# An mLSTM/Fourier backbone: adaLN weight loads, their products and h's tiles re-ordered in the first stage

## The chip, the cores and the metric

The kernel runs on 1 core of one Trainium2 chip, in one launch. The metric is device time in microseconds (us), from the runs of the whole program; the program before takes 1016.68 us (median of 3 runs, 1015.91 to 1017.34).

## The reference, cut to what matters

Two layers over 512 latent tokens `x` with a prefix of 256 context tokens `ctx`, width D = 1024, E = 2048. Everything is float32. The change touches only what leads to the input `h` of layer 0 and what shares its stage:

```python
sc_lat, sc_ctx = silu(c), silu(c_ctx)
sh, sc, g = split(sc_lat @ w_ada[0] + b_ada[0], 3)        # adaLN: shift, scale, gate; w_ada[0] is 1024 x 3072
h  = rmsnorm(x,   norm_g[0]) * (1 + sc)  + sh             # 512 x 1024
hc = rmsnorm(ctx, norm_g[0]) * (1 + scc) + shc            # 256 x 1024, from sc_ctx
xm, o_pre, z = split(h @ w_in, 3)                         # w_in: 1024 x 6144
q = einsum('bnhd,hde->bhne', xconv, w_q)                  # 4 heads of 512
k = einsum('bnhd,hde->bhne', xconv, w_k) * 512 ** -0.5
```

Behind it come the mLSTM scan in both directions, the output map, and a Fourier layer.

## The kernel before, in words

Matrix products in float32 are made of three products of rounded halves (`hi` x `hi`, `hi` x `lo`, `lo` x `hi`); `split` writes both halves of a tile (line 106 casts, line 107 subtracts).

The program's first stage, called M here, needs no token. For each head it forms M = w_q w_k^T / sqrt(512), so that q and k are never formed by themselves. It runs 16 steps `i` = (head h, quarter et). A step issues, in this order: at et = 3 `fold_sum(h)` (16 small products with gate weights); `turn` of the *next* step (8 TensorE transposes of w_q and w_k, copied by ScalarE, split by VectorE and POOL); then `product(h, et)` (12 matmuls of 128x512, lines 371 and 372). After each of the 12 matmuls `side_step` lets one piece of a list of side jobs run: `fold_turn` (4 transposes), `ada_done` (8 transposes), `h_tile(k)` (6 transposes of token tiles in two pieces, scale and shift by ScalarE, `split` of the context half and the latent half), `open_wp` (first weight split of the next stage).

Other work sits behind a step's product: `gate_weights` (8 transposes of m_w_if), `params` (3 transposes of the small vectors; it makes silT = silu(c), which the adaLN products read), `ada_part` (16 products of 4 rows of w_ada with silT, line 272; one half of the K range of one half of the 2048 columns, so four `ada_part` in all), the squares and norms of the tokens. Behind M comes stage X (`x_cols`, lines 497 to 504), which multiplies h with w_in and needs all eight h tiles in its first pass.

Loads: `sy.dma_start` runs on SyncE's queue (SP), in program order. A DMA takes one of eight semaphores, DMAHW0 to DMAHW7, and waits at its issue until the semaphore's last user has landed; a DMA into a buffer in use also waits there for the engine that reads the buffer. What stands behind waits too. The tag `wraw` has two buffers, which hold m_w_if first, then pieces of 1 MB of w_ada, then pieces of w_in; `adw` is one more buffer of 1 MB. w_q and w_k have two buffers per head.

The order of PE, DVE, ACT and POOL is that of the program text (`manual_schedule`); the order of SP is a scheduler's.

Of the kernel before, what the change touches and what calls it, by code (L numbers as in the profile page):

```python
# [9 lines left out]
F32 = mybir.dt.float32  # L10
# [14 lines left out]
H = 4  # L25
# [40 lines left out]
def hybrid_kernel(ctx: ExitStack, tc: tile.TileContext, I, out):  # L66
# [110 lines left out]
    def load_q(h, between=None):  # L177
        w = {nm: A1.tile([P, 4, DH], F32, tag=f"w{nm}", bufs=2, name=f"w{nm}") for nm in "qk"}
        for s_ in (slice(0, P), slice(P, 2 * P), slice(2 * P, DH)) if h == 0 else (slice(0, DH),):
            for nm in "qk":  # L180
                sy.dma_start(out=w[nm][:, :, s_], in_=I[f"m_w_{nm}"][0, h].rearrange("(t p) e -> p t e", p=P)[:, :, s_])
                if between:
                    between()
        wqk[h] = {nm: [w[nm][:, t] for t in range(4)] for nm in "qk"}
# [17 lines left out]
    bif = edge[0:NR, 2:4]  # L202
    gp.memset(bif, 0.0)

    def load_small(n):
        for _ in range(n):
            dst, src = rows_in.pop(0)
            sy.dma_start(out=dst, in_=src)
# [4 lines left out]
        for i in range(6):  # L213
            sy.dma_start(out=xs[i], in_=I["ctx"][0, i * P:(i + 1) * P, :] if i < 2 else I["x"][0, (i - 2) * P:(i - 1) * P, :])

    def ada_load(half, part):
        w = []
        for k in range(4 * part, 4 * part + 4, 2):
            if len(w) == 0 and part == 1:
                t = A2.tile([P, 2, D], F32, tag="adw", bufs=1, name="adw")  # L220
            else:
                t = wraw().rearrange("p (a k) c -> p a (k c)", a=2)
            sy.dma_start(out=t, in_=I["w_ada"][0, k * P:(k + 2) * P, half * D:(half + 1) * D].rearrange("(a p) c -> p a c", p=P))
            w += [t[:, 0], t[:, 1]]
            load_small(min(3, len(rows_in)))
        return w

    NG, BA, CB, LW, SK, CW = 16, 32, 80, 96, 112, 128

    def params():  # L230
# [65 lines left out]
    def h_tile(k):  # L296
        pl, pc = ps("gt", 2), tp()
        for i in range(2):
            tr(pc[:, i * P:(i + 1) * P], xs[i][:, k * P:(k + 1) * P])
        raw = A2.tile([P, NT], F32, tag="hraw", bufs=3, name="hraw")  # L300
        sc.activation(out=raw[:, 0:NCX], in_=pc[:, 0:NCX], func=AF.Identity,
                      scale=acol[:, 1, k, 1:2], bias=acol[:, 0, k, 1:2])
        for i in range(4):
            tr(pl[:, i * P:(i + 1) * P], xs[2 + i][:, k * P:(k + 1) * P])
            if i == 1:
                yield
        sc.activation(out=raw[:, NCX:], in_=pl, func=AF.Identity,
                      scale=acol[:, 1, k, 0:1], bias=acol[:, 0, k, 0:1])
# [50 lines left out]
    def side_step():  # L359
        while side and next(side[0], side) is side:  # L360
            side.pop(0)

    def product(h, et):

        if et == 0:
            pm[h] = [mm() for _ in range(4)]
        q, k = T.pop((h, "q", et)), T.pop((h, "k", et))
        for dt in range(4):
            c = slice(dt * P, (dt + 1) * P)
            for j, (l, r) in enumerate(((q[0], k[0]), (q[0], k[1]), (q[1], k[0]))):  # L370
                te.matmul(pm[h][dt], lhsT=l[:, c], rhs=r, start=(et == 0 and j == 0), stop=(et == 3 and j == 2))  # L371
                side_step()
        if et == 3:
            for dt in range(4):
                mst = A1.tile([P, DH], F32, tag="mst", bufs=4, name="mst")
                sc.activation(out=mst, in_=pm[h][dt], func=AF.Copy, scale=DH ** -0.5)
                m_st.append((h, dt, mst))
# [23 lines left out]
                         op=ALU.add, axis=mybir.AxisListType.X)  # L401
        yield

    load_q(1, lambda: load_small(3))
    st_st = ExitStack()
    st_st.enter_context(tc.manual_schedule(engines=ENGINES))
    w_in = I["m_w_in"][0]
    aw = {}
    warm = edge[:, 1:2]
    sc.activation(out=warm, in_=nhalf, func=AF.Sigmoid)  # L410
    b1_st, b2_st, b3_st = ExitStack(), ExitStack(), ExitStack()
# [1 line left out]
    def open_wp():  # L413
        nonlocal WP, w_bufs, w_first, w_split
        a2_st.close()
        WP = pool("WP", "left", stack=b1_st)
        w_bufs = 2
        w_split = wsplit([w_first[:, :, q * P:(q + 1) * P] for q in range(2)])
        w_first = [next(w_split)]
        yield  # L420

    steps = [(h, et) for h in range(H) for et in range(4)]
    turn(0, 0)
    for i, (h, et) in enumerate(steps):
        if et == 3:
            fs = fold_sum(h)
        if i + 1 < len(steps):
            turn(*steps[i + 1])
        if et == 3:
            side.append(fold_turn(h, fs))  # L430
        product(h, et)
        if et == 0:
            m_store()
        if i == 0:
            aw[0] = ada_load(0, 0)
            load_q(2)
        elif i == 1:
            gate_weights()
        elif i == 3:
            params()  # L440
        elif i == 4:
            ada_part(0, aw[0])
            aw[1] = ada_load(0, 1)
            load_x()
        elif i == 7:
            ada_part(1, aw[1])
            load_q(3)
            aw[2] = ada_load(1, 0)
            side.append(ada_done(0))
        elif i == 11:  # L450
            ada_part(0, aw[2])
            aw[3] = ada_load(1, 1)
            w_first = wraw()
            sy.dma_start(out=w_first, in_=w_in[:, 0:256].rearrange("(k p) c -> p k c", p=P))
            sy.dma_start(out=cst[:, P:], in_=I["cst"][:, P:])
            for r in range(2):
                for j, nm in enumerate(("m_b_i", "m_b_f")):
                    sy.dma_start(out=bif[32 * r:32 * r + H, j:j + 1], in_=I[nm][0, r, :].unsqueeze(1))
        elif i == 12:
            ada_part(1, aw[3])  # L460
            side.append(ada_done(1))
            side.extend(h_tile(k) for k in range(KD))
            side.append(open_wp())
        for j in {7: (0, 1), 8: (2,), 9: (3, 4), 10: (5,)}.get(i, ()):
            token_square(j)
        if i == 10:
            rstd_of(rs, ss, 1.0 / D)
        elif i in (11, 12):
            token_norms(3 * i - 33)
    m_store()  # L470
    while side:
        side_step()
# [1070 lines left out]
```

## Time and profile before

| | us |
|---|---|
| median of 3 runs | 1016.68 |
| lowest, highest | 1015.91, 1017.34 |
| the profiled execution | 1012.39 |
| its span, first to last instruction | 1010.6 |
| TensorE (PE) busy in the span | 982.0 (97%) |
| VectorE (DVE) busy | 736.4 (73%) |
| ScalarE (ACT) busy | 435.5 (43%) |
| POOL (GpSimd) busy | 137.0 (14%) |

How to read it: times inside the program are us from the span's start. The profiled execution took 1.8 us more than its span and 4.3 us less than the median of the runs. A row of the timeline gives start, busy time, engine, line, output <- inputs, how many, and in brackets how long the engine idled before and on whom. Matmuls overlap, so from one start to the next is the time that each costs. M runs from 0 to the first matmul of line 497.

### The profile page before, as it was taken

Reading aid. Unit: us, or ns where it says so; the run is one execution under the profiler, and the core shown is the slowest. Engines: PE = TensorE matmul, PEld = TensorE weight load, DVE = VectorE, ACT = ScalarE, POOL = GpSimd, SP = SyncE. Lnnn points to the kernel's source line nnn. Section 1 sums busy time; section 2 is a strip of 40 time slices with the busy share of each in tenths; the row PEclk is TensorE's granted clock in tenths of the full one; section 3 lists DMA queues with packets and bytes.
Section 4 is the critical chain, followed back from the end, with each engine's and each line's share of the span. In section 5 each row is a group of like instructions: output and inputs, shape, how many; then the busy total and the mean of one; then the engine's idle time right before and its main releaser. Section 6 shows DMA issues by size and latency. Waiting matters only on the chain.

```text
span 1010.6 us, 14164 instructions
## 1 busy us (share of the span) xinstructions
PE 982.0 (97%) x5231; PEld 805.5 (80%) x5231; DVE 736.4 (73%) x1303; ACT 435.5 (43%) x824; POOL 137.0 (14%) x126
## 2 busy tenths in 40 slices
PE   7999999999999998999999999999989999999997
PEld 6666888788888866787788888888868898988886
DVE  4558698898888757637888888775799876657623
ACT  2455434344344244236545455353666332325510
POOL 2003100000000000411535352110102101000000
PEclk9999999999999999999999999999999999999999
DMA  9963776657765474634354544453523443413602
GB/s 310 381 246 114 222 228 224 209 181 246 229 214 199 155 245 137 176 111 152 114 161 125 158 126 126 156 174 101 195 94 103 138 146 115 135 64 99 204 1 84
DMA packets 146893, 166.70 MB, mean 165 GB/s; under 512 B 15108, under 2 KB 107804, under 8 KB 146824
## 3 DMA queue, kind: packets, MB, share of 16 engines
q1 hardware_dynamic: 131172, 140.35, 43.9%
q10 hardware_dynamic: 15652, 25.45, 6.7%
q8 instruction: 41, 0.67, 0.3%
q14 instruction: 28, 0.23, 0.1%
HBM read 138.47 MB, written 27.30 MB: 164 GB/s over the span
## 4 chain that ended last, share of the span: by engine, by line
PE 73%; DVE 15%; issue 5%; ACT 3%; DMA 3%; POOL 1%; SPq 0%; ACTq 0%; POOLq 0%; DVEq 0%
PE mm L101 14%; PE mm L102 14%; PE mm L103 14%; PE tp L137 4%; PE mm L371 4%; PE gt L965 2%; PE mm L497 2%; PE mm L503 2%; PE mm L499 2%; PE gt L102 1%; PE gt L103 1%; PE gt L101 1%; PE mm L498 1%; PE mm L504 1%; PE mm L500 1%
## 5 line engine op out<-in xcount | busy, mean ns | idle before, releaser
L106 ACT CAST whi<-wraw 128x1024 fp32r<-128x1024 f32 x62 | 64.2, 1049 | 102.0 <-PE mm L102 42.3
L520 DVE SCALAR_TENSOR_TENSOR acc<-xm,pcol,acc 128x441 f32<-128x441 f32 (+2 forms) x128 | 89.0, 696 | 25.7 <-ACT acc L510 21.7
L107 DVE TENSOR_TENSOR wlo<-wraw,whi 128x1024 fp32r<-128x1024 f32 x60 | 76.0, 1280 | 41.3 <-ACT whi L106 39.9
L101 PE MATMUL mm<-hhi,whi 128*128 128x512 f32 x256 | 102.0, 398 | 1.3 <-ACT whi L106 1.3
L103 PE MATMUL mm<-hhi,wlo 128*128 128x512 f32 x256 | 100.4, 392 | 0.5 <-DVE wlo L107 0.5
L102 PE MATMUL mm<-hlo,whi 128*128 128x512 f32 x256 | 100.4, 392 | 0.0
L107 DVE TENSOR_TENSOR wol<-woraw,woh 128x512 fp32r<-128x512 f32 x80 | 55.1, 703 | 36.8 <-ACT woh L106 36.3
L102 PE MATMUL mm<-wol,yhi 128*128 128x512 f32 (+1 forms) x208 | 78.3, 376 | 2.1 <-DVE wol L107 2.1
L101 PE MATMUL mm<-woh,yhi 128*128 128x512 f32 (+1 forms) x208 | 78.5, 377 | 0.1
L103 PE MATMUL mm<-woh,ylo 128*128 128x512 f32 (+1 forms) x208 | 77.7, 373 | 0.0
L106 ACT CAST woh<-woraw 128x512 fp32r<-128x512 f32 x80 | 48.3, 619 | 42.9 <-PE mm L103 24.7
L101 PEld LDWEIGHTS mm<-hhi,whi 128*128 128x128 f32 x256 | 48.4, 189 | 13.5 <-ACT whi L106 1.7
L103 PEld LDWEIGHTS mm<-hhi,wlo 128*128 128x128 f32 x256 | 48.5, 189 | 11.5 <-DVE wlo L107 1.0
L102 PEld LDWEIGHTS mm<-hlo,whi 128*128 128x128 f32 x256 | 48.5, 189 | 9.4
L497 PE MATMUL mm<-hhi,whi 128*128 128x512 f32 x128 | 51.2, 400 | 0.0
L499 PE MATMUL mm<-hlo,whi 128*128 128x512 f32 x128 | 50.9, 398 | 0.0
L107 POOL TENSOR_TENSOR xhl<-st,xhh 128x768 fp32r<-128x768 f32 x16 | 34.5, 2171 | 114.3 <-ACT xhh L106 61.9
L101 PE MATMUL mm<-Zh,whi 128*128 128x512 f32 x128 | 50.0, 391 | 0.0
L102 PE MATMUL mm<-Zl,whi 128*128 128x512 f32 x128 | 50.0, 391 | 0.0
L103 PE MATMUL mm<-Zh,wlo 128*128 128x512 f32 x128 | 49.8, 389 | 0.0
L102 PEld LDWEIGHTS mm<-wol,yhi 128*128 128x128 f32 x208 | 39.2, 188 | 10.6 <-DVE wol L107 4.0
L503 PE MATMUL mm<-hhi,wlo 128*128 128x512 f32 x128 | 45.9, 398 | 0.0
(360 smaller groups left out, 2636.4 us busy)
## 6 DMA issues: line engine op xcount, KB each, us to landing
wraw<-in_m_w_in_dram SPq DMA_DIRECT2D x32, 512.0 KB, 6.5
adw<-in_w_ada_dram SPq DMA_DIRECT2D x32, 512.0 KB, 3.9
wraw<-in_f_w_in_dram SPq DMA_DIRECT2D x14, 1024.0 KB, 5.3
woraw<-in_m_w_out_dram SPq DMA_DIRECT2D x48, 256.0 KB, 2.8
wraw<-in_m_w_in_dram SPq DMA_DIRECT2D x8, 1024.0 KB, 5.6
g_d<-g ACTq DMA_DIRECT2D x32, 256.0 KB, 5.9
gg<-g_d SPq DMA_DIRECT2D x32, 256.0 KB, 2.7
woraw<-in_f_w_out_dram SPq DMA_DIRECT2D x32, 256.0 KB, 3.4
```

Of the source, the lines that this page charges most:

```text
L101: te.matmul(ps, lhsT=lh, rhs=rh, start=start, stop=False, **kw)
L102: te.matmul(ps, lhsT=lh, rhs=rl, start=False, stop=False, **kw)
L103: te.matmul(ps, lhsT=ll, rhs=rh, start=False, stop=stop, **kw)
L106: (sc.copy if he is None else he.tensor_copy)(out=hi, in_=src)
L107: (le or gp).tensor_tensor(out=lo, in0=src, in1=f32(hi), op=ALU.subtract)
L137: te.transpose(out_, in_=in_, identity=ident[0:n, 0:n])
L371: te.matmul(pm[h][dt], lhsT=l[:, c], rhs=r, start=(et == 0 and j == 0), stop=(et == 3 and j == 2))
L497: te.matmul(pl, lhsT=lh, rhs=hhi[k], start=(k == 0), stop=False)
L499: te.matmul(pl, lhsT=lh, rhs=hlo[k], start=False, stop=False)
L503: te.matmul(pl, lhsT=ll, rhs=hhi[k], start=False, stop=(k == KD - 1))
L520: ve.scalar_tensor_tensor(out=ag[:, r0:r1, o0:o1], in0=xg[:, r0 + dy:r1 + dy, o0 + dx:o1 + dx], scalar=tap(4 + 3 * dy + dx), in1=ag[:, r0: ...
L965: te.matmul(po, lhsT=k.ph[:, t], rhs=v, start=(t == 0 and v is s.v[0][0]), stop=False)
```

## The change

It does five things.

- Six products of a 128x128 tile of ones with itself run on PE at the very start (`WAKE`).
- The nine small loads go ahead of everything else behind m_w_if; then two pieces of w_ada; and only then w_q and w_k of head 1. `ada_load` loads one piece of 1 MB, not two, and is called where a buffer comes free.
- `gate_weights`, `params` and the four `ada_part` move to earlier steps: behind products 0, 1, and 2, 3, 5, 7 (before: 1, 3, and 4, 7, 11, 12). `ada_done` runs in steps 4 and 8 (before: 8 and 13).
- The eight `h_tile` run in steps 9 to 14 (before: 13 to 15), and the side jobs of a step are spaced evenly over its 12 matmuls, by their number `n`.
- All halves of h, and the `lo` half of the first w_in pieces, are written by DVE (before: half of the `lo` halves of h, and those of w_in, by POOL).

```diff
+WAKE = 6
...
     gp.memset(ones, 1.0)
+    awake = tp(P)
+    for _ in range(WAKE):
+        te.matmul(awake, lhsT=ones, rhs=ones, start=True, stop=True)
...
-    def ada_load(half, part):
-        w = []
-        for k in range(4 * part, 4 * part + 4, 2):
-            if len(w) == 0 and part == 1:
-                t = A2.tile([P, 2, D], F32, tag="adw", bufs=1, name="adw")
-            else:
-                t = wraw().rearrange("p (a k) c -> p a (k c)", a=2)
-            sy.dma_start(out=t, in_=I["w_ada"][0, k * P:(k + 2) * P, half * D:(half + 1) * D].rearrange("(a p) c -> p a c", p=P))
-            w += [t[:, 0], t[:, 1]]
-            load_small(min(3, len(rows_in)))
-        return w
-
+    def ada_load(half, part, i):
+
+        if part == 1 and i == 0:
+            t = A2.tile([P, 2, D], F32, tag="adw", bufs=1, name="adw")
+        else:
+            t = wraw().rearrange("p (a k) c -> p a (k c)", a=2)
+        k = 4 * part + 2 * i
+        sy.dma_start(out=t, in_=I["w_ada"][0, k * P:(k + 2) * P, half * D:(half + 1) * D].rearrange("(a p) c -> p a c", p=P))
+        aw.setdefault((half, part), []).extend((t[:, 0], t[:, 1]))
...
-        split(raw[:, 0:NCX], chi[k], clo[k], ve, ve if k % 2 else gp)
-        split(raw[:, NCX:], hhi[k], hlo[k], ve, gp if k % 2 else ve)
+        split(raw[:, 0:NCX], chi[k], clo[k], ve, ve)
+        split(raw[:, NCX:], hhi[k], hlo[k], ve, ve)
...
-    def product(h, et):
+    def product(h, et, n):
...
+        done = 0
...
                 te.matmul(pm[h][dt], lhsT=l[:, c], rhs=r, start=(et == 0 and j == 0), stop=(et == 3 and j == 2))
-                side_step()
+                while done < (3 * dt + j + 1) * n // 12:
+                    side_step()
+                    done += 1
+        while side:
+            side_step()
...
-    load_q(1, lambda: load_small(3))
+    load_small(9)
+    ada_load(0, 0, 0)
+    ada_load(0, 1, 0)
+    load_q(1)
...
-        w_split = wsplit([w_first[:, :, q * P:(q + 1) * P] for q in range(2)])
+        w_split = wsplit([w_first[:, :, q * P:(q + 1) * P] for q in range(2)], ve)
...
+    after = {
+        0: lambda: (gate_weights(), ada_load(0, 0, 1)),
+        1: lambda: params(),
+        2: lambda: (ada_first(0, 0), ada_load(0, 1, 1), ada_load(1, 0, 0), load_x()),
+        3: lambda: (ada_first(1, 0), ada_load(1, 0, 1), load_q(2), ada_load(1, 1, 0)),
+        5: lambda: (ada_first(0, 1), ada_load(1, 1, 1), [token_square(j) for j in range(3)]),
+        6: lambda: (load_q(3), [token_square(j) for j in range(3, 6)], rstd_of(rs, ss, 1.0 / D)),
+        7: lambda: (ada_first(1, 1), last_loads(), token_norms(0)),
+        8: lambda: token_norms(3),
+    }
+    turned = {9: (0,), 10: (1,), 11: (2,), 12: (3, 4), 13: (5,), 14: (6, 7)}
...
-        product(h, et)
+            n += 5
+        if i in (4, 8):
+            side.append(ada_done(i // 4 - 1))
+            n += 9
+        for k in turned.get(i, ()):
+            side.append(h_tile(k))
+            n += 2
+        product(h, et, n)
         if et == 0:
             m_store()
-        if i == 0:
-            aw[0] = ada_load(0, 0)
-            load_q(2)
-        elif i == 1:
-            gate_weights()
-        elif i == 3:
-            params()
-        elif i == 4:
-            ada_part(0, aw[0])
-            aw[1] = ada_load(0, 1)
-            load_x()
...
+        after.get(i, lambda: None)()
```

`ada_first(part, half)` calls `ada_part`; `last_loads` holds the loads of the first w_in piece and of the constants, which stood in the loop at i = 11.

What the change does to the order, in three places. Line numbers of the changed text are some 4 to 10 higher; a number behind a name is its buffer.

SP's queue, before, from the load of m_w_if on: `wq_159` and `wk_160` are w_q and w_k of head 1, `rows0` takes the small vectors, `wraw_232` is the first piece of w_ada.

```order
L189 DMA wraw_146<-in_m_w_if_dram 96x1024
L181 DMA wq_159<-in_m_w_q_dram 128x4x512
L208 DMA rows0_148<-in_c_dram 8x128
L208 DMA rows0_148<-in_c_ctx_dram 8x128
L208 DMA rows0_148<-in_norm_g_dram 16x128
L181 DMA wk_160<-in_m_w_k_dram 128x4x512
L208 DMA rows0_148<-in_b_ada_dram 48x128
L208 DMA rows0_148<-in_m_conv_b_dram 16x128
L208 DMA rows0_148<-in_m_ln_w_dram 16x128
L223 DMA wraw_232<-in_w_ada_dram 128x2x1024
```

The same queue in the changed kernel, from the fourth small load behind m_w_if on (`wraw_175`, `adw_177` and `wraw_261` are pieces of w_ada, `wq_179` and `wk_180` head 1):

```order
L212 DMA rows0_155<-in_b_ada_dram 48x128
L212 DMA rows0_155<-in_m_conv_b_dram 16x128
L212 DMA rows0_155<-in_m_ln_w_dram 16x128
L212 DMA rows0_155<-in_m_skip_dram 16x128
L212 DMA rows0_155<-in_m_conv_w_dram 128x128
L212 DMA rows0_155<-in_m_conv_w_dram 16x128
L227 DMA wraw_175<-in_w_ada_dram 128x2x1024
L227 DMA adw_177<-in_w_ada_dram 128x2x1024
L185 DMA wq_179<-in_m_w_q_dram 128x4x512
L185 DMA wk_180<-in_m_w_k_dram 128x4x512
L227 DMA wraw_261<-in_w_ada_dram 128x2x1024
L218 DMA xs0_158<-in_ctx_dram 128x1024
```

No large load stands between m_w_if and the last small one any more, and head 1 stands behind two pieces of w_ada.

PE, before, from the last matmul of product 2 on (`gt<-wqT,wif` is fold_sum, `tp<-cst,wq` the turn of step 4, which is head 1):

```order
L371 MATMUL mm<-wkTh,wqTl 128x512
L389 MATMUL gt<-wqT,wif 32x512 x4
L389 MATMUL gt<-wkT,wif 32x512 x4
L137 MATMUL tp<-cst,wq 128x128 x4
L137 MATMUL tp<-cst,wk 128x128 x4
```

PE in the changed kernel from the same matmul on:

```order
L375 MATMUL mm<-wkTh,wqTl 128x512
L275 MATMUL gt<-wraw,silT 32x512 x8
L397 MATMUL gt<-wqT,wif 32x512 x4
L397 MATMUL gt<-wkT,wif 32x512 x4
L138 MATMUL tp<-cst,wq 128x128 x4
L138 MATMUL tp<-cst,wk 128x128 x4
```

The first `ada_part`, which reads `wraw_175` and `wraw_261`, now stands ahead of fold_sum and of the turn of head 1.

PE in step 14, before: between two matmuls of the product stand pieces of `h_tile` (`xs`), a tile every second matmul.

```order
L371 MATMUL mm<-wkTh,wqTl 128x512
L137 MATMUL gt<-cst,xs_155 128x128
L137 MATMUL gt<-cst,xs_156 128x128
L371 MATMUL mm<-wkTh,wqTh 128x512
L137 MATMUL tp<-cst,xs_151 128x128
L137 MATMUL tp<-cst,xs_152 128x128
L137 MATMUL gt<-cst,xs_153 128x128
L137 MATMUL gt<-cst,xs_154 128x128
L371 MATMUL mm<-wkTl,wqTh 128x512
```

PE in the changed kernel, in step 12, one of the two steps with two tiles:

```order
L138 MATMUL tp<-cst,xs_158 128x128
L138 MATMUL tp<-cst,xs_159 128x128
L138 MATMUL gt<-cst,xs_160 128x128
L138 MATMUL gt<-cst,xs_161 128x128
L375 MATMUL mm<-wkTh,wqTh 128x512
L375 MATMUL mm<-wkTl,wqTh 128x512
L375 MATMUL mm<-wkTh,wqTl 128x512
L138 MATMUL gt<-cst,xs_162 128x128
L138 MATMUL gt<-cst,xs_163 128x128
L375 MATMUL mm<-wkTh,wqTh 128x512
L375 MATMUL mm<-wkTl,wqTh 128x512
L375 MATMUL mm<-wkTh,wqTl 128x512
```

Three matmuls stand between two pieces of a tile, and a tile takes six.

## Rows read from the trace of the kernel before

**Rows 1.** Windows: length, busy us by engine, granted PE clock, DMA share, GB/s.
```profile
20.00:60.00 40.00, 40.00 (x247) 28.02 (x246) 23.51 (x46) 19.87 (x37) 0.00 (x0) 1.00 1.00 389
95.00:96.00 1.00, 1.00 (x8) 0.00 (x0) 0.97 (x2) 0.00 (x0) 1.00 (x2) 0.50 0.00 0
```

**Rows 2.** Timeline of PE, regular steps of M and a late adaLN product.
```profile
56.74 0.60 PE L137 MATMUL tp<-cst,wq 128*128 128x128 f32 x4
...
59.93 0.39 PE L371 MATMUL mm<-wkTl,wqTh 128*128 128x512 f32 x1
60.15 0.39 PE L371 MATMUL mm<-wkTh,wqTl 128*128 128x512 f32 x1
60.47 1.06 PE L389 MATMUL gt<-wqT,wif 128*32 128x512 f32 x8
...
62.33 0.65 PE L137 MATMUL tp<-cst,wq 128*128 128x128 f32 x4
...
66.57 1.93 PE L272 MATMUL gt<-wraw,silT 128*32 128x512 f32 x16
...
72.22 1.05 PE L272 MATMUL gt<-adw,silT 128*32 128x512 f32 x4
...
76.18 0.66 PE L137 MATMUL tp<-cst,wq 128*128 128x128 f32 x4
```

**Rows 3.** Timeline of PE, the end of M and stage X.
```profile
80.33 0.38 PE L137 MATMUL tp<-cst,xs 128*128 128x128 f32 x2
...
85.01 0.38 PE L137 MATMUL tp<-cst,xs 128*128 128x128 f32 x2
...
86.14 0.38 PE L137 MATMUL tp<-cst,xs 128*128 128x128 f32 x2
...
93.05 1.94 PE L389 MATMUL gt<-wqT,wif 128*32 128x512 f32 x8 [1.82 <-ACT hraw L307]
...
96.49 0.50 PE L371 MATMUL mm<-wkTh,wqTh 128*128 128x512 f32 x1
...
100.14 0.39 PE L497 MATMUL mm<-hhi,whi 128*128 128x512 f32 x1
...
142.69 0.38 PE L498 MATMUL mm<-chi,whi 128*128 128x256 f32 x1 [0.40 <-ACT acc L510]
```

**Rows 4.** The tile hhi: durations in ns, min/median/max.
```profile
L106 DVE CAST hhi<-hraw x8: 418/472/1519, 82.2 to 98.1; 128x512 fp32r<-128x512 f32 x8
```

**Rows 5.** Timeline of SP's queue: when loads are issued.
```profile
11.97 0.31 SPq L208 DMA_DIRECT2D rows<-in_m_conv_b_dram  x1
13.41 0.31 SPq L208 DMA_DIRECT2D rows<-in_m_ln_w_dram  x1
15.75 0.39 SPq L223 DMA_DIRECT2D wraw<-in_w_ada_dram  x1
...
16.68 0.89 SPq L208 DMA_DIRECT2D rows<-in_m_conv_w_dram  x2
18.33 0.38 SPq L223 DMA_DIRECT2D wraw<-in_w_ada_dram  x1
...
21.10 0.37 SPq L181 DMA_DIRECT2D wk<-in_m_w_k_dram  x1
```

**Rows 6.** DMA issues between 33.0 and 33.5: size, us from issue to landing.
```profile
wraw<-in_w_ada_dram SPq DMA_DIRECT2D x1, 1024.0 KB, 5.1
```

**Rows 7.** Timeline of PE, the first steps of M.
```profile
10.26 0.63 PE L371 MATMUL mm<-wkTh,wqTh 128*128 128x512 f32 x1
10.69 0.53 PE L371 MATMUL mm<-wkTl,wqTh 128*128 128x512 f32 x1
...
16.30 1.02 PE L137 MATMUL gt<-cst,wraw 96*128 96x96 f32 x8
...
20.88 1.07 PE L389 MATMUL gt<-wqT,wif 128*32 128x512 f32 x8
...
26.89 0.54 PE L137 MATMUL tp<-cst,rows 128*128 128x128 f32 x3
```

More of the change, by code (lines that the diff above doesn't have):

```diff
@@ L214, in load_x @@
             sy.dma_start(out=xs[i], in_=I["ctx"][0, i * P:(i + 1) * P, :] if i < 2 else I["x"][0, (i - 2) * P:(i - 1) * P, :])
-    def ada_load(half, part):
-        w = []
-        for k in range(4 * part, 4 * part + 4, 2):
-            if len(w) == 0 and part == 1:
-                t = A2.tile([P, 2, D], F32, tag="adw", bufs=1, name="adw")
-            else:
-                t = wraw().rearrange("p (a k) c -> p a (k c)", a=2)
-            sy.dma_start(out=t, in_=I["w_ada"][0, k * P:(k + 2) * P, half * D:(half + 1) * D].rearrange("(a p) c -> p a c", p=P))
-            w += [t[:, 0], t[:, 1]]
-            load_small(min(3, len(rows_in)))
-        return w
+    def ada_load(half, part, i):
[6 more added lines that the diff above has]
+        aw.setdefault((half, part), []).extend((t[:, 0], t[:, 1]))
+    aw = {}
     NG, BA, CB, LW, SK, CW = 16, 32, 80, 96, 112, 128
@@ L407, in hybrid_kernel @@
     w_in = I["m_w_in"][0]
-    aw = {}
     warm = edge[:, 1:2]
@@ L417, in open_wp, with ada_first, last_loads @@
         w_bufs = 2
-        w_split = wsplit([w_first[:, :, q * P:(q + 1) * P] for q in range(2)])
+        w_split = wsplit([w_first[:, :, q * P:(q + 1) * P] for q in range(2)], ve)
         w_first = [next(w_split)]
         yield
+    def ada_first(part, half):
+        ada_part(part, aw.pop((half, part)))
+    def last_loads():
+        nonlocal w_first
+        w_first = wload(w_in, 0)
+        sy.dma_start(out=cst[:, P:], in_=I["cst"][:, P:])
+        for r in range(2):
+            for j, nm in enumerate(("m_b_i", "m_b_f")):
+                sy.dma_start(out=bif[32 * r:32 * r + H, j:j + 1], in_=I[nm][0, r, :].unsqueeze(1))
+    after = {
[9 more added lines that the diff above has]
+    turned = {9: (0,), 10: (1,), 11: (2,), 12: (3, 4), 13: (5,), 14: (6, 7)}
     steps = [(h, et) for h in range(H) for et in range(4)]
@@ L428, in hybrid_kernel @@
             turn(*steps[i + 1])
+        n = 0
+        if i == 15:
+            side.append(open_wp())
+            n += 1
         if et == 3:
             side.append(fold_turn(h, fs))
-        product(h, et)
+            n += 5
[6 more added lines that the diff above has]
+        product(h, et, n)
         if et == 0:
             m_store()
-        if i == 0:
-            aw[0] = ada_load(0, 0)
-            load_q(2)
-        elif i == 1:
-            gate_weights()
-        elif i == 3:
-            params()
-        elif i == 4:
-            ada_part(0, aw[0])
-            aw[1] = ada_load(0, 1)
-            load_x()
[L445 to L469, printed above, removed]
+        after.get(i, lambda: None)()
     m_store()
```

## The prediction, made before the changed kernel ran

> **What bounds the kernel now.** I read the windows first. TensorE (PE) is busy throughout 20 to 60 us, and so are the DMA engines: share 1.00, 389 GB/s [rows 1]. So two things bound the first half of M at once, and a transfer that comes later there may be seen by PE. Then I read PE's timeline for the price of each piece of M. A turn and 12 matmuls take 60.47 - 56.74 = 3.73; one matmul 60.15 - 59.93 = 0.22, say 0.23 with what rounding hides; so a turn 3.73 - 12 x 0.23 = 0.97. The 16 products of fold_sum take 62.33 - 60.47 = 1.86, and an `ada_part` has 16 of the same shape. The step with the turning of fold takes 66.57 - 62.33 = 4.24 [rows 2].
>
> Where M loses time shows at two places. The last `ada_part` stands from 72.22 to 76.18, 3.96 instead of 1.86: it waits 2.10 for its weights [rows 2]. And the end of M: from 80.33 to the first matmul of X at 100.14 it takes 19.81 [rows 3]. What is left to do at 80.33: two matmuls 0.46, step 14 3.73, fold_sum 1.86, step 15 without a turn 4.24 - 0.97 = 3.27, and eight h tiles. A tile costs (86.14 - 85.01) - 0.46 = 0.67 [rows 3], so 5.36. That is 14.68; 5.13 is lost. The reasons are visible: PE waits 1.82 on ACT's hraw before 93.05 [rows 3], the granted clock then is 0.50, the 1.2 GHz level [rows 1], and fold_sum takes 96.49 - 93.05 = 3.44 instead of 1.86. So 1.58 of the 5.13 is the clock. Behind it are the splits of h: the cast of hhi takes between 418 and 1519 ns [rows 4].
>
> Behind 100.14 PE idles 0.40 once in the next 50 us [rows 3], so what M gains or loses passes nearly whole to the end.
>
> **The change part by part, without the loads.** If all weights were there in time, the spread of h's tiles would give back the 5.13 and the earlier products the 2.10. VectorE (DVE) takes over POOL's halves: a tile then costs it about 0.42 + 0.69 + 0.28 + 0.42 = 1.8 (an estimate: the 418 ns cast [rows 4], a subtraction of the same width at some 0.7, and half as wide the two of the context), against the 3.73 + 0.67 that PE needs for a step with one tile. In steps 12 and 14, with two tiles, DVE has 3.6 and the turn's splits of about 2.2, 5.8 against PE's 3.73 + 1.34 = 5.07; it is 0.7 behind and catches up in step 13, where the splits of a turn are needed only a step later. I cost it at nothing. The covering work is the product in between; without it 0.7 in each of the two steps would show. The lo half of w_in on DVE has the same cover. Norms and squares move on ACT and DVE under PE's products: nothing. The six products on ones lie ahead of the first weights, in time where PE has nothing to do; at best they raise the clock and give back 0.2 for each of the first four or five matmuls, whose starts are 10.69 - 10.26 = 0.43 apart [rows 7] instead of 0.22; about 1. That is hidden by the next wait, so I take 0.
>
> **The loads.** SP's rows say how a load waits: a small one issued at 13.41 waited for m_w_if, the piece of w_ada at 15.75 for head 1's w_q, the piece at 18.33 for its w_k, the load at 21.10 for the first piece [rows 5]. So loads of 1 MB land in the order of issue, (21.10 - 15.75) / 2 = 2.67 apart, and the queue never ran empty, because head 1 was already in it.
>
> Now head 1 stands behind the small loads, and these each wait for a semaphore. The load of conv_w waits for m_w_if, 13.41; two issues take 0.89 [rows 5]; the first piece of w_ada is issued at 14.30. Until then only small loads are in the queue: it runs dry. A piece issued to a nearly idle queue lands 5.1 later [rows 6], at 19.4. Four of 1 MB follow: second piece, w_q, w_k, third piece: 4 x 2.67 = 10.7. The third piece lands at L = 30.1. This takes m_w_if as late as before, though w_q of head 1 no longer runs beside it. It can't land ahead of w_k of head 0, which is seen at 11.97 [rows 5]; that end gives L = 28.7. I take the middle, 29.4, as nothing decides between the ends.
>
> When does PE ask for it? `gate_weights` now stands behind product 0 and needs m_w_if, 13.41. From 16.30 to 20.88 such an interval of gate_weights, turn and product took 4.58; params 0.54 [rows 7]; turn and product 2 another 3.73 [rows 2]: 22.3. There stands the first `ada_part`, and behind it, in PE's order, fold_sum and all else. PE waits from 22.3 to L, some 7 us. (Head 1's w_k lands at L - 2.67, so the turn behind would wait too.) All gains ahead of it are lost in it, the warm clock and the earlier start.
>
> **The sum.** In the profiled execution M needed 100.14 - 20.88 = 79.26 from the end of product 2. Less params 0.54, the waits 2.10 and 5.13: 71.49. An idle stretch of 7 us brings the clock down, as a shorter one did before 93.05; 1.58 more [rows 1, 3]. X starts at L + 73.07 = 102.5, against 100.14: +2.3. The 0.40 that PE waited in X [rows 3] may go, as weights come no later: +1.9. The span's neighbour, the profiled execution's own 1012.39, becomes 1014.3; the median of the runs shown is 4.3 above that execution, and I forecast against it: 1016.68 + 1.9 = 1018.6. With L at its ends +1.2 to +2.6. A measurement of this kernel tells about 0.2%, 2.0 us, from no change.
>
> **A page against it.** The rows give 5.1 for a lone load of 1 MB and 2.67 for each behind another [rows 5, 6]. The Trainium skill, page "DMA: Bandwidth & Descriptors", section "Anatomy of one DMA — SWDGE (gpsimd) path", fits 2.0 us plus bytes over 436 GB/s, measured on another issuing path than SP's; as an estimate from that page 4.4 and 2.4, L = 28.3 and +0.8 in all. The rows are slower than the page here, and decide.
>
> **Rivals.** *Faster.* The wait before the first `ada_part` is short, because the loads get through sooner than in order at 2.67. Each us of L is a us. With L below 25 the sum is -2.1 or better, and with L at 22.3 or less there is no idle stretch and no lost clock: X at 22.3 + 71.49 = 93.8, 1016.68 - 6.3 = 1010.4. For it: the 5.13 and 2.10 are real, and the middle of M has no other wait. Against it: 7.6 MB are ahead of that point, and [rows 5] show the order. Chance 0.24.
>
> *The loads close up.* m_w_if lands at 11.97 and the loads follow 18.33 - 15.75 = 2.58 apart [rows 5]: L = 12.86 + 5.1 + 10.3 = 28.3, +0.8, 1017.5. Chance 0.18. By the Trainium skill's page "DMA: Bandwidth & Descriptors", the section above, the sum would come out about there.
>
> *A second wait behind the first.* From L to the last `ada_part`, PE has 1.86 + 1.58, fold_sum 1.86, 4.24, 1.86, a step with ada_done of about 4.7, 3.73, 1.86, 3.73, 1.86 and 4.24: 31.5 [rows 2, 3]. In that time 3 MB of tokens, five pieces of w_ada, head 2 and a stored product, 11 MB, have to land: 29.4 at 2.67, and some 2 more because the next piece is issued only when the first `ada_part` frees its buffer, 3.4 behind L, and takes 5.1. 31.4 against 31.5: no slack. At 10% more per load PE waits 3 more: +4.9, 1021.6. Chance 0.19.
>
> *DVE binds in the last steps*, 0.7 in two steps and a little in X: +1.5 more, 1020.1. Chance 0.03.
>
> **How the numbers follow.** The forecast, L between 28.7 and 30.1, has 0.36, half of it beyond 2.0 us. Slower: 0.18 + 0.19 + 0.03 = 0.40. Same: 0.18 + 0.18 = 0.36. Faster 0.24. The range 1012.0 to 1022.5 reaches over half into the faster case and past the second wait; the forecast's own is 1017.9 to 1019.3. I leave out a tenth at each end.
>
> **What would show it.** Right: in PE's timeline a wait of 5 to 8 us on a DMA at the products of line 275 near 22, the end of it near 29; a dip of the DMA share near 14 to 16; granted clock 0.50 behind the wait; the last `ada_part` without a long wait; no wait on hraw in steps 9 to 15; X starting at 101.5 to 103. Wrong: no wait near 22, or X before 98. A wait at the third or fourth `ada_part` would be the second rival's; DVE busy without a pause in steps 12 to 15 and PE waiting for wqTh or wkTh the last one's.

## The result, and the profile of the changed kernel

The changed kernel takes 1022.75 us (median of 5 runs, 1020.81 to 1023.19); the kernel before, run beside it, 1015.91 (5 runs, 1012.68 to 1017.34). The ratio is 1.0071, 95% interval 1.0046 to 1.0096: slower by 0.7%. The forecast was 1018.6, range 1012.0 to 1022.5. Slower was its likeliest sign, but the loss is 6.8 us where 1.9 were forecast, and it lies 0.25 us outside the range.

The loss that can be placed is in M. The first matmul of stage X starts at 106.88 us instead of 100.14 [rows 3], 6.74 later, and the medians are 6.84 apart. (The spans of the two profiled executions, 1021.0 and 1010.6, differ by more. Over all 12 profiles of this study what lies behind X's start takes 910.2 to 914.6 us, without a relation to the edits: the changed kernel and e3 below have the same program there, and it takes 914.1 and 910.3. So I compare starts of X.)

First the windows of the changed kernel, with the columns of [rows 1]:

```profile
13.00:16.00 3.00, 3.00 (x21) 2.67 (x20) 0.84 (x4) 0.03 (x1) 0.00 (x0) 1.00 0.37 61
...
27.00:30.00 3.00, 0.00 (x0) 0.00 (x0) 0.00 (x0) 0.00 (x0) 0.00 (x0) 0.58 1.02 418
30.00:34.00 4.00, 2.88 (x14) 0.73 (x18) 0.69 (x1) 0.00 (x0) 0.00 (x0) 0.50 0.75 307
```

Between 13 and 16 the DMA engines move 61 GB/s; in the kernel before they move 404 GB/s there. From 27 to 30 PE does nothing while they run full. Behind that the clock is 0.50. PE's timeline shows what it waited for, and how little came of the early adaLN products:

```profile
23.38 1.05 PE L275 MATMUL gt<-wraw,silT 128*32 128x512 f32 x4
31.12 3.49 PE L275 MATMUL gt<-wraw,silT 128*32 128x512 f32 x12 [6.68 <-DMA wraw<-in_w_ada_dram]
33.84 1.62 PE L397 MATMUL gt<-wqT,wif 128*32 128x512 f32 x8
...
36.25 0.66 PE L138 MATMUL tp<-cst,wq 128*128 128x128 f32 x4
...
62.42 0.62 PE L275 MATMUL gt<-adw,silT 128*32 128x512 f32 x2
...
64.28 0.66 PE L138 MATMUL tp<-cst,wq 128*128 128x128 f32 x4
...
84.25 0.60 PE L138 MATMUL tp<-cst,wq 128*128 128x128 f32 x4
...
85.77 0.50 PE L375 MATMUL mm<-wkTh,wqTh 128*128 128x512 f32 x1 [0.48 <-ACT mst L384]
...
87.71 0.44 PE L138 MATMUL tp<-cst,xs 128*128 128x128 f32 x2 [0.97 <-ACT wqT L327]
...
91.17 0.60 PE L138 MATMUL tp<-cst,wq 128*128 128x128 f32 x4
...
93.89 0.44 PE L138 MATMUL tp<-cst,xs 128*128 128x128 f32 x2 [0.31 <-ACT wqT L327]
...
95.99 0.60 PE L138 MATMUL tp<-cst,wq 128*128 128x128 f32 x4
...
102.91 0.50 PE L375 MATMUL mm<-wkTh,wqTh 128*128 128x512 f32 x1
...
104.56 0.30 PE L138 MATMUL gt<-cst,fsb 128*128 128x128 f32 x1 [0.45 <-ACT mst L384]
...
106.88 0.40 PE L505 MATMUL mm<-hhi,whi 128*128 128x512 f32 x1
```

Four of the first product's 16 matmuls run, then PE stands 6.68 us for the third piece of w_ada. The last adaLN product, which waited 2.10 before [rows 2], starts at 62.42 and ends 1.86 later: that wait is gone. SP's queue shows the cause, as the small loads and the pieces are issued:

```profile
13.45 0.83 SPq L212 DMA_DIRECT2D rows<-in_m_conv_w_dram  x2
14.32 0.42 SPq L227 DMA_DIRECT2D wraw<-in_w_ada_dram  x1
...
16.86 2.02 SPq L227 DMA_DIRECT2D wraw<-in_w_ada_dram  x1
```

The third piece lands 14.2 us behind its issue at 16.86, with 4 MB ahead of it. And the end of M has waits that were not there before: 0.48, 0.97 and 0.31 between 85 and 94 us, in the rows above. ScalarE's (ACT's) timeline shows what they wait for:

```profile
84.45 0.78 ACT L310 ACTIVATE hraw<-gt,small 128x512 f32<-128x512 f32 x1
85.13 2.05 ACT L384 ACTIVATE mst<-mm 128x512 f32<-128x512 f32 x4
87.04 0.62 ACT L327 COPY wqT<-tp 128x512 f32<-128x512 f32 x1
...
91.37 1.83 ACTq L389 DMA_DIRECT2D m_d<-mst  x4
93.25 0.59 ACT L327 COPY wqT<-tp 128x512 f32<-128x512 f32 x1 [1.10 <-issue]
```

ACT scales the finished head's four tiles into `mst` behind the scaling of an h tile, all four at once when the head's product has ended, and only then copies w_q for the next turn; the next product needs the PSUM buffer that the first of the four frees (0.48), and PE's next tile the one that the copy frees (0.97). A step later the issue of the stores of these four tiles, on ACT's queue, delays the same copy again (0.31).

### The profile page after: what moved, and what is told of

It reads as the page before. It is cut to its first block, busy times and chain, and to the rows that moved or that the text cites. A ratio compares the mean times of both kernels' runs of the same rounds, so it can differ in the third digit from the quotient of the medians.

```text
span 1021.0 us, 14188 instructions
## 1 busy us (share of the span) xinstructions
PE 985.7 (97%) x5243; PEld 808.4 (79%) x5243; DVE 741.0 (73%) x1313; ACT 435.8 (43%) x824; POOL 122.8 (12%) x116
## 4 chain that ended last, share of the span: by engine, by line
PE 61%; DVE 16%; issue 6%; ACT 3%; DMA 3%; POOL 1%; ACTq 0%; POOLq 0%; SPq 0%; DVEq 0%
PE mm L103 13%; PE mm L102 13%; PE mm L104 13%; PE mm L505 2%; PE mm L511 2%; PE mm L507 2%; PE tp L138 2%; PE gt L973 2%; DMA woraw<-in_m_w_out_dram 1%; PE mm L506 1%; PE mm L512 1%; PE mm L508 1%; PE gt L550 1%; DVE acc L528 1%; DVE wol L108 1%
## 5 line engine op out<-in xcount | busy, mean ns | idle before, releaser
L108 DVE TENSOR_TENSOR wlo<-wraw,whi 128x1024 fp32r<-128x1024 f32 x62 | 79.2, 1292 | 39.4 <-ACT whi L107 39.4
L108 POOL TENSOR_TENSOR xhl<-st,xhh 128x768 fp32r<-128x768 f32 x16 | 31.8, 2004 | 116.5 <-ACT xhh L107 62.5
```

## The experiments

The start of X is from one profile of each kernel; the wait is that for the third piece of w_ada, and "L" is where it ends. Ratios are to the kernel before, run beside each. By how much a kernel is later than the one before agrees between the starts of X and the medians within 0.9 us, except in e5, whose profile has X 2.43 later and whose median is 0.6 earlier. Each profile is of one of the runs, for e4, e7 and e10 of the fastest.

| kernel | L | X starts | median | ratio, 95% interval |
|---|---|---|---|---|
| changed | 31.12 | 106.88 | 1022.75 | 1.0071, 1.0046 to 1.0096 |
| e1, head 1 first | 28.38 | 105.83 | 1020.52 | 1.0056, 1.0035 to 1.0077 |
| e2, no tile at a head's end | 29.36 | 104.49 | 1019.25 | 1.0046, 1.0028 to 1.0064 |
| e3, no ones | 29.81 | 108.31 | 1021.85 | 1.0071, 1.0046 to 1.0097 |
| e4, early loads, later products | none | 101.06 | 1015.59 | 1.0009, 0.9998 to 1.0021 |
| e5, full queue | none | 102.57 | 1014.84 | 1.0000, 0.9986 to 1.0015 |
| e6, later products only | none | 109.83 | 1025.53 | 1.0099, 1.0072 to 1.0126 |
| e7, wait filled | 29.78 | 104.33 | 1019.24 | 1.0040, 1.0025 to 1.0055 |
| b1, before with VectorE's splits | none | 99.16 | 1014.55 | 0.9994, 0.9979 to 1.0008 |
| e8, before's front, late half of the change | none | 106.43 | 1021.11 | 1.0067, 1.0046 to 1.0088 |
| e10, the same two steps later | none | 94.32 | 1010.35 | 0.9959, 0.9942 to 0.9975 |

### Head 1 first

```diff
-    load_small(9)
+    load_q(1, lambda: load_small(3))
+    load_small(3)
     ada_load(0, 0, 0)
     ada_load(0, 1, 0)
-    load_q(1)
```

> Only the order of loads is undone: head 1 and its small loads in between stand behind m_w_if again, the first two pieces of w_ada behind them; the same 5 MB stand ahead of the third piece. Theory (the dry queue between 13.5 and 16.5 us delays everything behind it): the third piece lands at 18.3 + 3 x 2.6 = 26.1 to 26.8 instead of 31.1, PE waits some 3 us from 23.4 instead of 6.7 behind the four products it can do, stage X starts at 101.5 to 103 instead of 106.9, time about 1018. Rival (the bytes ahead of the third piece set its landing, the pause in the queue is made up): it lands within 1 us of 31.1, X within 1 us of 106.9, time 1022 to 1023.

Neither came out. The third piece lands at 28.38, 2.7 earlier than in the changed kernel's profile and 1.0 to 1.4 earlier than in the three other kernels with its loads (e2, e3, e7), but not at 26.5, and X gains only 1.05. The pause in the queue was moved, not undone: the six small loads behind w_k hold the first piece back until 16.90, and the DMA share in 15 to 18 us is 0.70. SP's queue in this kernel: w_k of head 1, the small load issued 2.5 behind the one before it, and that piece:

```profile
7.62 0.39 SPq L185 DMA_DIRECT2D wk<-in_m_w_k_dram  x1
...
15.61 0.31 SPq L212 DMA_DIRECT2D rows<-in_m_skip_dram  x1
...
16.90 0.42 SPq L227 DMA_DIRECT2D wraw<-in_w_ada_dram  x1
```

Of the 2.74 gained at L, 1.34 go to the clock, which stays low longer (the 12 matmuls and fold_sum take 34.85 - 28.38 = 6.47 instead of 36.25 - 31.12 = 5.13), and 0.35 to the last adaLN product, which takes 2.21. 2.74 - 1.34 - 0.35 = 1.05.

### No tile at a head's end

```diff
-    turned = {9: (0,), 10: (1,), 11: (2,), 12: (3, 4), 13: (5,), 14: (6, 7)}
+    turned = {9: (0, 1), 10: (2, 3), 13: (4, 5), 14: (6, 7)}
```

> Only the table of h tiles differs: two tiles each in steps 9, 10, 13, 14, none in 11 and 12. Theory (in steps 11 to 13 ScalarE's queue is what PE waits for: the tile's scale and shift stand ahead of the four copies of the finished head, and the turn's copies behind them): the waits of 0.48, 0.97 and 0.31 us between 85 and 94 us go, X starts about 2 us earlier, at 104.9, time about 1020.8. Rival (VectorE binds, 0.7 us per step with two tiles): the waits come back in steps 9 to 11 and 13 to 15, X starts within 0.5 us of 106.9.

The theory held. In step 11 ACT now scales the four tiles one by one as the product's quarters end, the last at 85.18, and the copy of w_q stands right behind:

```profile
85.18 0.60 ACT L384 ACTIVATE mst<-mm 128x512 f32<-128x512 f32 x1 [0.21 <-PE mm L375]
85.67 0.58 ACT L327 COPY wqT<-tp 128x512 f32<-128x512 f32 x1
```

None of the three waits between 84 and 96 us is left; only that of 0.45 at step 15 is. From the turn behind the last adaLN product to X it takes 104.49 - 64.29 = 40.20, in the changed kernel 106.88 - 64.28 = 42.60: 2.40 less. VectorE with two tiles a step did not bind ahead of step 15. (The edit takes tiles out of both steps, 11 and 12; no run takes out one alone.)

The same profile shows the second wait of the rivals. L came 1.76 earlier, by no part of the edit, and yet both kernels turn at 64.28 and 64.29, because the last adaLN product then waits for its own piece. PE's timeline of this kernel; the third row is the start on that piece, 1.07 behind the first half's:

```profile
29.36 3.63 PE L275 MATMUL gt<-wraw,silT 128*32 128x512 f32 x12 [7.57 <-DMA wraw<-in_w_ada_dram]
...
61.38 1.05 PE L275 MATMUL gt<-adw,silT 128*32 128x512 f32 x4
62.45 0.62 PE L275 MATMUL gt<-wraw,silT 128*32 128x512 f32 x2
```

### No ones

```diff
-WAKE = 6
+WAKE = 0
```

> Only the six products on ones are left out. Theory (the wait for the third piece ends when it lands, whatever PE did before): X starts within 0.3 us of 106.9, time 1022 to 1023.5. Rival (they bring the clock up for the first products, and that reaches the end): the first product's matmuls take 0.43 us each for longer, X starts 0.5 to 1 us later.

The times agree with the theory: 1021.85, the same ratio. The profile does not tell the two apart. X starts 1.4 later although the third piece lands 1.3 earlier: behind the wait the 12 matmuls and fold_sum take 6.23, 1.10 more than in the changed kernel, w_q's copy in step 13 is late by 1.39 instead of 0.31, behind 2.91 us of store issues on ACT's queue, and the last adaLN product takes 0.62 more. The first product's matmuls are 0.43 us apart until 11.24; with the ones, in the changed kernel, until 13.68. So the ones did not warm that execution. In e1, e2, e4, e6 and e7, with the same ones, that product's matmuls are 0.23 to 0.24 apart from 9.3 us on at the latest, and of the five kernels without ones only e10's are; so they may help, but a gain of theirs is nowhere to be seen in the time.

### Early loads, later products

The first loads are those of the run with head 1 first; of the rest:

```diff
     after = {
         0: lambda: (gate_weights(), ada_load(0, 0, 1)),
         1: lambda: params(),
-        2: lambda: (ada_first(0, 0), ...
+        2: lambda: load_q(2),
+        3: lambda: (ada_first(0, 0), ada_load(0, 1, 1), ada_load(1, 0, 0), load_x()),
+        5: lambda: (ada_first(1, 0), ada_load(1, 0, 1), ada_load(1, 1, 0)),
...
```

> Head 1 first as in the run with that order; head 2 ahead of the tokens; the four adaLN products behind steps 3, 5, 7, 8 instead of 2, 3, 5, 7, ada_done in steps 6 and 9, tiles in steps 10 to 14 with that of step 11 ahead of the turning of fold and one in step 12. Theory (both losses of the changed kernel are order alone: loads that come late, and ScalarE's queue at a head's end): no long wait at the adaLN products, X starts at 23.4 + 71.5 = 94.9 to 97, time 1011 to 1013. Rival (the DMA engines bound the first half of M whatever the order): a wait of 3 us or more at one of the adaLN products, X at 99 or later, time 1015 or more.

Most of the loss is gone: 1015.59, the interval holds 1. The long wait is not there, but smaller ones are, each behind a DMA or ACT: `gate_weights`, behind step 0, now has head 1 beside its load and stands 3.03 us, as PE's timeline shows:

```profile
14.28 1.21 PE L138 MATMUL gt<-cst,wraw 96*128 96x96 f32 x8 [3.03 <-DMA wraw<-in_m_w_if_dram]
```

With head 1 beside it m_w_if landed at 13.14 (e1) and 14.28, with the queue left empty at 11.72 to 12.85 (e2, e7, e6), where PE waited 0.25 to 1.31 for it. X at 101.06 lies outside the theory's 94.9 to 97 and is the rival's figure; but the rival's wait of 3 us at an adaLN product is not there, the longest is 0.65.

### Full queue

```diff
-        0: lambda: (gate_weights(), ada_load(0, 0, 1)),
-        1: lambda: params(),
+        1: lambda: (gate_weights(), ada_load(0, 0, 1), load_q(2), load_x(0)),
+        2: lambda: params(),
...
```

> As the run with early loads and later parts, with the queue kept full: behind m_w_if w_q of head 1, three small loads, w_k, the first piece of w_ada, the six other small loads, the second piece; gate_weights behind step 1 as before the change, params behind step 2; head 2 and half of the tokens ahead of the pieces that wait for a buffer; tiles two each in steps 10, 11 (ahead of the turning of fold), 13, 14, none in 12. Theory (each loss seen so far is an order: the dry queue, m_w_if asked for too early, ScalarE's queue at a head's end): no wait over 1 us at gate_weights or at an adaLN product, clock 1.00 from 12 to 95 us, stage X starts at 94 to 97, time 1009 to 1012. Rival (the DMA engines bound the first half of M, so that a wait taken away comes back at the next load): at least 3 us of waits for DMAs between 12 and 70 us, X at 99 or later, time 1014 or more.

The rival held. PE waits for head 0's w_k until 9.38 in this execution (2.47), for the small loads at 23.25 (0.78), for the second adaLN product's piece at 42.57 and the last one's at 64.21 (0.68); the last three make 3.86. The longest of the waits for adaLN weights, in PE's timeline:

```profile
42.57 0.62 PE L275 MATMUL gt<-wraw,silT 128*32 128x512 f32 x2 [2.40 <-DMA wraw<-in_w_ada_dram]
```

The DMA share is 1.01 to 1.06 from 25 to 55 us. This order of loads wins nothing over the kernel before; that no order could, with the products asking this early, one run does not show.

### Later products only

The changed kernel's first loads, the products behind steps 3, 5, 7, 8. Head 2's load moves with them, to behind the second product and one more piece.

> The changed kernel's order of the first loads (head 1 behind two pieces, the dry queue) with the later places of the adaLN products (steps 3, 5, 7, 8) and the tiles of the run with the full queue. Theory (the first adaLN product is only the first that waits; head 1 lands 2.6 us ahead of the third piece and is late too): PE now waits at the turn of head 1, from 23 to 25 on until 27 to 28.5, 3 to 4 us, and not at the adaLN product behind it; X at 100 to 102, time about 1016. Rival (the early place of the adaLN product is the whole cause): no wait over 1 us between 20 and 35 us, X below 97.

The slowest of all, 1025.53. What the theory says of head 1 is there: PE waits 1.55 and 1.84 for it, to 27.83. What it left out is that head 2, behind the tokens and two pieces, is late in its turn, 4.67 and 1.40. The four waits in PE's timeline:

```profile
25.36 0.63 PE L138 MATMUL tp<-cst,wq 128*128 128x128 f32 x4 [1.55 <-DMA wq<-in_m_w_q_dram]
27.83 1.08 PE L138 MATMUL tp<-cst,wk 128*128 128x128 f32 x4 [1.84 <-DMA wk<-in_m_w_k_dram]
...
55.45 1.12 PE L138 MATMUL tp<-cst,wq 128*128 128x128 f32 x4 [4.67 <-DMA wq<-in_m_w_q_dram]
57.97 1.12 PE L138 MATMUL tp<-cst,wk 128*128 128x128 f32 x4 [1.40 <-DMA wk<-in_m_w_k_dram]
```

The place of the first adaLN product is therefore not the cause by itself: with the queue run dry, head 1 is late where the third piece is not. The wait for head 2 says less, as the edit itself moved that load back.

### The wait filled

```diff
-        2: lambda: (ada_first(0, 0), ...
+        2: lambda: (idle_ones(26), ada_first(0, 0), ...
```

> The changed kernel with 26 more products on ones ahead of the first adaLN product, which fill most of PE's wait there (about 0.24 us each, 6.3 us) and compute nothing that is used. Theory (the idle wait costs its length and, behind it, matmuls at the lower clock, 1.9 to 3.5 us in the runs so far): the granted clock stays 1.00 to 36 us, the adaLN product's last 12 matmuls and fold_sum take 1.4 + 1.86 instead of 2.7 + 2.4, X starts 1.9 to 3 us earlier measured from the landing of the third piece, 72.5 to 74 behind it instead of 75.8. Rival (the clock is not what is lost; the time behind the wait is set by later loads): X starts 75 to 76 us behind the landing, as in the changed kernel.

The clock stays at 1.00, and the matmuls behind the wait run at full speed. The windows of this kernel:

```profile
27.00:30.00 3.00, 1.37 (x10) 0.30 (x12) 0.00 (x0) 0.00 (x0) 0.00 (x0) 1.00 1.02 418
30.00:34.00 4.00, 4.00 (x33) 1.17 (x26) 1.74 (x3) 0.00 (x0) 0.00 (x0) 1.00 0.52 161
```

And its PE timeline behind the wait:

```profile
29.78 1.91 PE L275 MATMUL gt<-wraw,silT 128*32 128x512 f32 x12 [1.63 <-DMA wraw<-in_w_ada_dram]
31.62 1.07 PE L397 MATMUL gt<-wqT,wif 128*32 128x512 f32 x8
...
33.48 0.66 PE L138 MATMUL tp<-cst,wq 128*128 128x128 f32 x4
```

From L to the turn it takes 33.48 - 29.78 = 3.70, in the changed kernel 5.13: against that the clock cost 1.43 there, and 2.0 to 2.8 in e1 to e3. X starts 74.55 behind L instead of 75.76; 1.43, less 0.23 more at the last adaLN product. Smaller than the theory's 1.9 to 3, and not nothing.

### Before, with VectorE's splits

```diff
-        split(raw[:, 0:NCX], chi[k], clo[k], ve, ve if k % 2 else gp)
-        split(raw[:, NCX:], hhi[k], hlo[k], ve, gp if k % 2 else ve)
+        split(raw[:, 0:NCX], chi[k], clo[k], ve, ve)
+        split(raw[:, NCX:], hhi[k], hlo[k], ve, ve)
```

> The kernel before with one part of the change: both halves of all h tiles are written by VectorE. Theory (POOL's subtractions, which hold hraw longer and beside which a cast of hhi took up to 1.52 us, make most of the 5.1 us lost at the end of M): the casts of hhi stay below 0.5 us, the wait of 1.82 us at 93 and the lower clock behind it go, X starts 2 to 3.5 us earlier, at 97 to 98, time about 1012. Rival (VectorE, crowded there, then binds instead: eight tiles at 1.8 us plus the turns in 20 us): PE waits as long as before, X at 99.5 to 101, time unchanged.

The tile hhi in this kernel, durations in ns (min/median/max):

```profile
L106 DVE CAST hhi<-hraw x8: 412/420/427, 82.2 to 99.1; 128x512 fp32r<-128x512 f32 x8
```

And PE's timeline where fold_sum of the last head begins:

```profile
92.09 1.07 PE L389 MATMUL gt<-wqT,wif 128*32 128x512 f32 x8 [1.28 <-ACT hraw L307]
```

The casts are short now, against 1519 ns at most [rows 4], and the clock does not fall: fold_sum takes 1.07 and not 1.94 for its first eight [rows 3]. But the wait is only shorter, 1.28 for 1.82, and a new one of 1.49 on VectorE's `fsb` stands at step 15. X gains 0.98, between theory and rival; the time cannot be told from before. Crowded tiles cost nearly as much on VectorE alone.

### The late half of the change alone, and the same two steps later

Both keep the kernel before up to the second adaLN product and move the last two: from behind steps 11 and 12 to 8 and 9 (e8), or to 10 and 11 (e10). Tiles from step 11 or 12 on, splits on VectorE, side jobs spaced by `n`.

```diff
-        elif i == 11:
-            ada_part(0, aw[2])
+        elif i == 8:
+            ada_part(0, aw[2])
...
-        elif i == 12:
-            ada_part(1, aw[3])
+        elif i == 9:
+            ada_part(1, aw[3])
```

> The kernel before with its own first loads, gate_weights, params and first two adaLN products, and of the change only what comes late: the third and fourth adaLN product behind steps 8 and 9 instead of 11 and 12, ada_done in steps 8 and 10, the h tiles in steps 11 (two, ahead of the turning of fold), 12 (one, in its last third), 13 (two) and 14 (three), all their splits on VectorE, side jobs spaced over the product. Theory (the late half of the change is worth having, the early half is what costs, because the DMA engines are full until 55 us): no wait over 0.5 us before the third adaLN product at 53, waits of about 1 us there and 1 to 1.5 us at the fourth, none over 0.5 us behind them; stage X starts at 95 to 97, time 1010.5 to 1012.5. Rival (the losses at the end of M only move: the waits for the last two pieces of w_ada grow to 3 us or more, or VectorE or ScalarE binds in steps 13 to 15): X at 98.5 or later, time 1014 or more.

The rival held. The third adaLN product waits twice, for each of its pieces, and the clock falls (0.54 in 59 to 63 us); step 15 then waits 2.98 for VectorE behind three tiles. PE's timeline:

```profile
55.46 1.59 PE L272 MATMUL gt<-wraw,silT 128*32 128x512 f32 x4 [2.00 <-DMA wraw<-in_w_ada_dram]
59.06 3.63 PE L272 MATMUL gt<-wraw,silT 128*32 128x512 f32 x12 [2.02 <-DMA wraw<-in_w_ada_dram]
...
103.28 0.30 PE L137 MATMUL gt<-cst,fsb 128*128 128x128 f32 x1 [2.98 <-DVE fsb L397]
```

Step 8's product ended at 53.46, and the turn behind the adaLN product begins at 62.62: 9.16 for 1.86 of work. The second of its pieces was there at 59.06. In the kernel before, step 10's product ends at 60.47, just behind that [rows 2], and so the next run put the adaLN product there:

```diff
-        elif i == 8:
+        elif i == 10:
             ada_part(0, aw[2])
...
-        elif i == 9:
+        elif i == 11:
             ada_part(1, aw[3])
...
-    jobs = {11: (0, 1), 12: (2,), 13: (3, 4), 14: (5, 6, 7)}
+    jobs = {12: (0,), 13: (1, 2, 3), 14: (4, 5, 6), 15: (7,)}
```

> As the run with the front of the kernel before and the late spread, with the last two adaLN products two steps later: behind steps 10 and 11 (before the change: 11 and 12), ada_done in step 12, h tiles one at the end of step 12, three in 13, three in 14, one in 15 ahead of the first weight split. Theory (an adaLN product is worth moving just so far that its pieces have landed and the next piece, issued when it is done, lands before the next one asks): no wait over 0.5 us at the four products, clock 1.00 from 12 us on; VectorE has 21 us of work from 74.3 on, so X starts at 95.5 to 97.5; time 1010.5 to 1012.5. Rival (what is saved at the adaLN products is lost to VectorE's eight tiles in three steps, as before the change): PE waits 3 us or more for VectorE's or ScalarE's results in steps 13 to 15, X at 98.5 or later, time 1014 or more.

PE's timeline of this kernel:

```profile
59.05 1.92 PE L272 MATMUL gt<-wraw,silT 128*32 128x512 f32 x16
60.93 1.07 PE L394 MATMUL gt<-wqT,wif 128*32 128x512 f32 x8
...
76.94 0.44 PE L137 MATMUL tp<-cst,xs 128*128 128x128 f32 x2 [1.26 <-ACT wqT L324]
...
92.45 0.30 PE L137 MATMUL gt<-cst,fsb 128*128 128x128 f32 x1 [1.03 <-DVE fsb L397]
```

All 16 matmuls of the third product run without a wait, and so do those of the fourth. X starts at 94.32, 5.8 earlier than before and 12.6 earlier than in the changed kernel: 1010.35 (9 runs, 1007.85 to 1013.63), 0.4% faster than the kernel before, with 1 outside the interval, and a little better than the theory's bounds. It beats both kernels. (The profile is of the fastest of the nine; the medians are 5.0 apart. The adaLN products, the spread of the tiles and VectorE's splits were moved together, and only the splits were also run alone, with 0.98 at X.) Two waits stand at the end of M, 1.26 and 1.03, together under the rival's 3.

## Why the prediction was right in sign and wrong in size

X's start was forecast at 102.5 and is 106.88, 4.4 later. By the steps of the sum:

- **L: the chain was right, its size 1.7 short.** Forecast 29.4, between 28.7 and 30.1; measured 31.12. In the four kernels that issue the same loads up to there (changed, e2, e3, e7) the first piece is issued at 14.32, 12.57, 13.25 and 13.11, 0.87 or 0.88 behind the issue that waits for m_w_if, and the wait ends 16.80, 16.79, 16.56 and 16.67 later. The sum had 5.1 + 10.7 = 15.8 for these five loads, about 1.0 too little; the other 0.7 is m_w_if, which landed as late as at the forecast's upper end (14.30), and I took the middle. The dry stretch is there.
- **When PE asks**: 23.38, forecast 22.3. It changes nothing, as said; the wait is 6.68 behind the four matmuls.
- **The clock**: forecast 1.86 + 1.86 + 1.58 = 5.30 for the adaLN product and fold_sum behind L; measured 5.13, with four matmuls done ahead of the wait. e7 puts the clock's part at 1.43. Right here; in e1 to e3 it was more.
- **"I cost it at nothing" is the step that failed.** The spread of h's tiles was weighed against VectorE alone. ACT was dismissed in half a sentence, for norms and squares. Steps 12, 13 and 15 take 6.92, 4.82 and 3.97 instead of 5.07, 4.40 and 3.27: 2.97 lost. e2 shows that steps 12 and 13, 2.27 of it, are the tile in step 11 and those in step 12 around the four `mst` copies and the stores. In ACT's order the last tile of step 11 stands ahead of all four copies, and they ahead of the copies for the next turn. The change had also moved the adaLN product away from behind step 11; but e2 has none there either and loses nothing, so that cover was not what was missing. The remaining 0.70 in step 15 is `fsb`, which VectorE copies behind tile 7. The profile names `mst`, which ended just before, at 104.51; but in all eleven kernels that wait there PE starts 0.82 to 0.84 us behind the start of the `fsb` copy, while the `mst` copy starts anywhere from 0.07 to 0.72 ahead of it, in e8 3.6. VectorE's timeline of the changed kernel:

```profile
103.73 0.68 DVE L400 COPY fsb<-gt 128x512 f32<-128x512 f32 x1
```

- 1.7 - 0.17 + 2.97 = 4.5, against 4.4 measured. Undoing the tiles alone does not bring the forecast back: in e2, with L at 29.36 as forecast, X starts 75.13 behind L, not 73.07. Of these 2.06, 1.05 are the second wait below, 0.40 the clock, and 0.45 the wait for `fsb`.
- **X's own wait**: 0.40 was to go [rows 3]; it is 1.1 at the same place, 0.7 more. Why, no run here settles.
- **The second wait** had a chance of 0.19 and "no slack". It did not show in the changed kernel, whose L was late, but in e1 to e3: their last product's piece comes 33.0 us behind L each time (61.39 - 28.38, 62.45 - 29.36, 62.83 - 29.81), where 31.4 had been reckoned (in e7, with no slow matmuls behind L, 59.90 - 29.78 = 30.1). The last product then takes 0.35, 1.05 and 0.62 longer than its 1.86. "Each us of L is a us" did not hold there: with the lower clock this is why an earlier L hardly helped e1. The rival's mechanism is real, its price, 3 on top of the forecast, too high by far.
- **Faster** (0.24) and **the loads close up** (0.18) fell: nothing landed ahead of its order, and in e2, where m_w_if had landed at 11.70, L was 29.36 and not 28.3.
- **DVE binds** (0.03, +1.5): its mechanism is seen at step 15, 0.7.

The sign came from the mechanism that was forecast, the wait behind the dry queue. The gain that was there to be had, 5.13 + 2.10, was real: e10's profile takes 5.8 of it. Without any idle stretch X was reckoned at 93.8 and is 13.1 later: the changed kernel lost 10.2 of that to its early half, up to the turn at 36.25, and 2.9 to the spread of the tiles.

## What to carry to other kernels

Where PE and the DMA engines are both full, a consumer may be moved ahead only to the point where its data has landed, and that point is read from the landings, not from when the operands' buffers are free: two steps too early cost 7.3 us in e8 (9.16 less 1.86). When work is put into a step, ask what it will stand ahead of in the order of every engine: here a tile's scaling ahead of ACT's four copies at a head's end, and these ahead of a copy that PE needs. Small loads that each wait for a semaphore empty a queue (61 GB/s from 13 to 16 us, 404 with head 1 between them); keep a large one between them.

## What the runs showed of the hardware

- After the idle stretch ahead of the third piece the granted clock was 0.50, and what it cost against e7 varies: 1.4 us in the changed kernel, 2.0 in e2, 2.5 in e3 and 2.8 in e1, for idle stretches of 4.0 to 7.6 us, the longest not the dearest. Products on ones in the wait kept it at 1.00.
- A VectorE cast beside a POOL subtraction waited for it whole. In e10 one cast of `hhi` takes 2630 ns and the others 420; it starts at 92.89, and POOL's subtraction of w_in's `lo` half runs from 92.56 for 2.68 us. The tile hhi in that kernel:

```profile
L106 DVE CAST hhi<-hraw x8: 420/420/2630, 75.2 to 92.9; 128x512 fp32r<-128x512 f32 x8
```

The Trainium skill, page "SBUF — State Buffer", section "SBUF: two separate sides", calls the port pair that the two share an exclusive lock, held for the whole instruction: the trace agrees.
- Stores issued by ACT cost it time in its own order: four issues took 1.83 us in the changed kernel and 2.91 in e3, and the copy behind them waited.
- The same loads landed up to 1.8 us apart from one execution to the next (L of 29.36 to 31.12), nearly as much as the whole forecast. Nearly all of it was there at m_w_if, whose landing let the next loads go at 11.70 to 13.45; from the first piece's issue on the four kernels agree within 0.24.
